# A hybrid S5, attention and memory block on one core: where S5's working tiles lie, and four rooms for raw weights in the memory stage

## Chip, core and metric

The kernel runs on one core of a Trainium2 chip. The metric is the device time of one execution in microseconds, the median of several runs. Lower is better.

The engines are named as in the profile: PE is TensorE's matmul, PEld its weight load, DVE is VectorE, ACT is ScalarE, POOL is GpSimd, and SP is the queue of SyncE from which almost every DMA of this kernel is issued. All five run their own instructions in order and wait for one another through semaphores.

## What is computed

One decoder layer on a sequence of 512 tokens, width 2048, all in float32:

```
h    = rmsnorm(x, norm_pre)
proj = h @ w_in          # columns: S5 input u, S5 gate, q, k, v, gate of the
                         # differential attention, query and gate of the memory attention
y_s  = s5_scan(u, ...)   # 64 groups of 16 channels, 64 complex states each
y_s  = gelu(y_s); y_s *= sigmoid(y_s @ w_glu + b_glu); y_s *= silu(gate_s)
y_d  = diff_attention(rope(q), rope(k), v) * silu(gate_d)
mem_n = rmsnorm(mem, norm_mem)                       # 256 memory tokens
y_x  = memory_attention(q_x, mem_n @ w_mem_kv) * silu(gate_x)
out  = x + rmsnorm(concat(y_s, y_d, y_x) @ w_out, norm_post)
```

`s5_scan` is a recurrence over the sequence, x_t = a x_(t-1) + b u_t with a complex diagonal a, read out as Re(C x) + D u.

## The kernel before

**Chunks.** All large products are cut into 144 *chunks*. A chunk is one block of weights of 128x1024 floats (512 KB) with the matmuls that use it. Every product is done as three matmuls on split operands: `parts` turns the raw block into a high half (`whi`, a cast on ACT) and a low half (`wlo`, a subtraction on DVE); activations are split the same way into `hhi`/`hlo`, `mhi`/`mlo` (the memory tokens), `ysh`/`ysl` and so on. A full chunk is 24 matmuls of 512 columns. The chunks of the memory stage are half as long: 24 matmuls of 256 columns (`w_kv_a`, eight chunks) or 12 of 512 (`w_kv_b`, eight chunks).

The chunks come in this order:

| chunks | from name | work |
|---|---|---|
| 0-15 | | S5 input u |
| 16-31 | S0 = 16 | keys and values of the memory tokens, the *memory stage* |
| 32-63 | SG = 32 | S5 gate, memory query, memory gate; S5 itself runs beside them |
| 64-71 | S1 = 64 | GLU |
| 72-87 | S2 = 72 | v and gate of the differential attention; memory attention beside them |
| 88-103 | S3 = 88 | k and q, differential attention beside them |
| 104-119 | S4 = 104 | first half of the output projection |
| 120-143 | S5 = 120 | second half, as a product with fewer block multiplications |

**Rooms for weights.** `load` puts a raw block into a tile of tag `raw`, of which there are two. `parts` makes `whi` and `wlo`, three of each. The main loop at the end of `tile_hybrid_block` runs the chunks; before the matmuls of chunk n it calls `load` up to chunk n + 3 and `parts` up to chunk n + 2 (from n = 9 on). A load into a room waits until the `wlo` of the block that was there is done.

**Side work.** Everything else hangs on the chunks through `at_slot(t, f)`: f is traced in chunk t + 0.75 by quarters, so that `at_slot(33.5, f)` comes after the second quarter of chunk 34. The matmuls keep the traced order exactly. DVE and ACT instructions traced after a `parts` call may not overtake it (class `After`). Otherwise a scheduler orders each queue at build time by traced order and by when it takes an instruction to be ready, so a load whose room is free can be put some chunks ahead of its place.

**S5.** The 64 groups are done in eight *octets* of eight groups. In the chunks before 32, `s5_products`, `s5_maps` and `s5_weights` prepare the parameters of every octet and write them to DRAM (`sp_dr`, `k_dr`); they load `bc`, an octet's B and C parameters. u lies in DRAM in `u_dr`. Then, for octet o, with e = SG + 1 + 3.25 o as its base slot:

- `s5_load` brings `sp` (576 KB), `s5_u` brings `us` for two octets in eight DMAs of 64 KB, `s5_toeplitz` brings `tm`;
- `s5_angles` makes cosine and sine (`cs`) on POOL, DVE and ACT; `s5_spread` copies a part of `sp` into the block matrices `ub` on ACT (four copies);
- `s5_states`, in six steps, does 16 matmuls of `us` and `ub` into `ps_s`, then a chain on DVE: rotations through `ra` into `wre` and `wim`, scans into `zre` and `zim`, rotations back into `x`;
- `s5_outputs` does 8 matmuls of `us` and `tm` and 16 of `x` and `sp` into `ps_t`, and then GELU.

The first octet has slots of its own: its states begin at e + 1.5, while those of the others begin at e.

**Memory on the right side.** Tiles of a stage come from pools that are stacked at the high end of SBUF. `mp` holds the memory stage's tiles: first `mhi` and `mlo` (16 KB per partition each, at 147,072 and 163,456), behind them `rmb`, parameters, `rows`, small tiles, the two `mT` tiles in which raw memory tokens arrive (`mem_load`), `mk` and `mv`. `s5_open` (slot SG - 1, the end of chunk 31) closes `mp` and opens `s5w` on the same memory, from 151,648 to 220,320. There the order of the allocations sets the addresses: `ub0`, `ub1`, `tm0`, `x0`, `tm1`, `x1`, then tags `sp`, `us`, `cs`, `ra`, `wre`, `wim`, `zre`, `zim`, `ysb`, `sq`. With `reuse_waits="tile"` a new tile waits for the old tiles that it overlaps, for each of them until its last use. `mhi` and `mlo` are read until the last matmul of chunk 31.

**Two later places.** `x_open` (slot S2 - 1) loads the memory attention's keys and values, `mk_dr` and `mv_dr`, through the two `raw` rooms and splits them. `ys_load(c)` loads two blocks of S5's finished output at slots S4 - 0.75 + c, splits them, and subtracts halves (`n3f`). The differential attention of the last head still runs there; `a_finish` transposes a head's result into `ps_t` and splits it into `ydh` and `ydl`.

Of the kernel before, what the change touches and what calls it, by code (L numbers as in the profile page):

```python
# [10 lines left out]
F32 = mybir.dt.float32  # L11
# [43 lines left out]
def tile_hybrid_block(ctx: ExitStack, tc: tile.TileContext, a: dict, out: bass.AP):  # L55
# [539 lines left out]
    def s5_open():  # L595
        prstack.close()
        mstack.close()
        wk = s5["wk"] = right_pool(s5stack, "s5w")
        s5["ub"] = [wk.tile([P, 4, 2, 64], F32, name=f"ub{i}") for i in range(2)]
        s5["d"] = []  # L600
        for i in range(2):
            d = {"tm": wk.tile([P, 8, P], F32, name=f"tm{i}"), "x": wk.tile([P, 8, NCH + 1], F32, name=f"x{i}")}
            g.memset(d["tm"], 0.0)
            g.memset(d["x"][:, :, 0], 0.0)
            g.memset(s5["ub"][i], 0.0)
            s5["d"].append(d)

    oct_ = [{} for _ in range(8)]

    def t512(tag, bufs=1, shape=(P, 512)):  # L610
        return s5["wk"].tile(list(shape), F32, tag=tag, name=tag, bufs=bufs)

    def s5_load(o):

        sp = t512("sp", 2, (P, 1152))
        sy.dma_start(sp, sp_dr[o])
        oct_[o].update(dp=sp[:, 0:640].rearrange("p (g j h) -> p g j h", g=8, h=16), up=sp[:, 640:1152])

    def s5_u(i, x):

        if x == 0:
            us = t512("us", 2, (P, 8, NCH))
            for k in range(2):
                oct_[2 * i + k]["us"] = us[:, 4 * k:4 * k + 4]
            s5["us"] = us
        src = u_dr[i].rearrange("(q x h) (s c) -> s x h q c", x=2, h=16, s=LCH)
        for b_ in range(LCH):
            r0 = 64 * x + 16 * b_
            sy.dma_start(s5["us"][r0:r0 + 16], src[LCH - 1 - b_, x])
# [9 lines left out]
    def s5_angles(o):  # L639

        cs = t512("cs", 2, (P, 2, 4, P))
# [17 lines left out]
    def s5_states(o):  # L659
# [17 lines left out]
        yield  # L677
        zre, zim = t512("zre"), t512("zim")
        for q in range(4):
# [6 lines left out]
        for i, (y1, y2, op) in enumerate(((zre, zim, ALU.subtract), (zim, zre, ALU.add))):  # L686
            b1, b2 = t512("ra", 2), t512("ra", 2)
            v.tensor_tensor(b1, y1, c_, ALU.mult)
            v.tensor_tensor(b2, y2, s_, ALU.mult)
            for g_ in range(2):  # L690
                rows = slice(64 * g_, 64 * g_ + 64)
                b1_, b2_ = (t_[rows].rearrange("p (q c) -> p q c", q=4) for t_ in (b1, b2))
                v.tensor_tensor(xg[64 * i:64 * i + 64, :, g_, 1:], b1_, b2_, op)
            yield

    def s5_outputs(o):
# [41 lines left out]
    for o in range(8):  # L738
        e = SG + 1 + 3.25 * o
        at_slot(e - 0.75, lambda o=o: s5_angles(o))  # L740
        at_slot(e - 0.5 + (0 if o else 1), lambda o=o: s5_spread(o))
        for i in range(6):
            at_slot(e + STEPS[i] + (0 if o else 1.5), lambda o=o, i=i: (oct_[o].setdefault("st", s5_states(o)), next(oct_[o]["st"])))
        if o > 1:
            at_slot(e - 2.5, lambda o=o: s5_load(o))
            if o % 2 == 0:
                for x in range(2):
                    at_slot(e - 3.25 + 0.75 * x, lambda o=o, x=x: s5_u(o // 2, x))
                    at_slot(e - 4.5 + 0.75 * x, lambda o=o, x=x: s5_toeplitz(o // 2, x))
        at_slot(e + 3.75, lambda o=o: s5_outputs(o))  # L750
    S5_END = SG + 1 + 3.25 * 7 + 4.5
# [49 lines left out]
    def x_open():  # L801
# [589 lines left out]
```

## Time and profile before

| | |
|---|---|
| median of 3 runs | 810.77 us (809.38 to 811.61) |
| the profiled execution | 813.09 us, span 811.3 us |
| mean granted TensorE clock | 0.988 |
| PE busy | 788.2 us, 97% of the span |
| DVE, ACT, POOL busy | 73%, 47%, 10% |
| HBM traffic | 216 GB/s over the span |
| the chain that ended last | PE 73%, DVE 10%, DMA 8%, ACT 4% |

The profile cuts the span into 40 slices and gives busy shares in tenths. PE's 97% says that little is left beside its own work, but a busy PE is not always a fast one: the profile also gives the clock granted to TensorE, and a matmul of 512 columns starts every 0.23 us at the full clock and every 0.43 us behind a longer wait. Matmul rows overlap: a row is 0.39 us long while the next one starts after 0.23, so times are taken from start to start. All instructions that the wrapper `After` issues carry line 71 in the profile and all matmuls line 96, so they are told apart by their tiles.

### The profile page before, as it was taken

To read this page: it belongs to the slowest core of one execution; us is meant where nothing else is said; L and a number is where in the kernel's file an instruction comes from. 1 tells how busy PE (TensorE), PEld (TensorE's weight loads), DVE (VectorE), ACT (ScalarE), POOL (GpSimd) and SP (SyncE) were. 2 spreads that over 40 slices of the span, in tenths; PEclk is the share of its full clock that TensorE was granted. 3 is DMA by queue.
4 is the path that set the end of the run, shared out by engine and by line. 5 is a ranking of instruction groups with operands and counts; after the bars stand their busy time and mean duration, and the time that the engine had idled before them with its cause. 6 is when DMAs were issued, how large, how long until landed. Compare 5 with 4: busy or idle time off the path is not lost.

```text
span 811.3 us, 10986 instructions
## 1 busy us (share of the span) xinstructions
PE 788.2 (97%) x3934; PEld 653.6 (81%) x3934; DVE 590.3 (73%) x1086; ACT 381.4 (47%) x621; POOL 80.3 (10%) x106
## 2 busy tenths in 40 slices
PE   8999999897999999999999999999999999999995
PEld 7888897685888888888887888888888788888884
DVE  5599987538898989856894554557988956775757
ACT  5654433332544445434633443445767644345631
POOL 0000000200000000000121222222211010000001
PEclk9999999898999999999999999999999999999998
DMA  8967876673465655357778766455653425437877
GB/s 262 368 253 260 278 238 228 218 203 93 149 170 147 158 160 147 129 144 243 238 233 271 256 159 179 156 157 181 157 130 104 134 101 182 156 108 242 298 286 259
DMA packets 66918, 158.87 MB, mean 196 GB/s; under 512 B 13616, under 2 KB 26800, under 8 KB 65200
## 3 DMA queue, kind: packets, MB, share of 16 engines
q1 hardware_dynamic: 64048, 141.39, 53.6%
q0 software_dynamic: 2816, 16.78, 8.3%
q8 instruction: 31, 0.51, 0.3%
q14 instruction: 23, 0.19, 0.1%
HBM read 134.68 MB, written 40.24 MB: 216 GB/s over the span
## 4 chain that ended last, share of the span: by engine, by line
PE 73%; DVE 10%; DMA 8%; ACT 4%; issue 3%; SPq 1%; POOL 0%; DVEq 0%; POOLq 0%; ACTq 0%
PE ps_mm L96 59%; PE ps_t L96 7%; PE ps_s L96 6%; DVE wlo L71 3%; ACT whi L71 2%; DMA raw<-in_w_kv_b_dram 2%; DMA raw<-in_w_in_a_dram 2%; PE ps_t L99 1%; DMA raw<-in_w_kv_a_dram 1%; SPq L71 1%; DMA ys_dr<-tg 1%; DMA sp<-sp_dr 1%; DMA raw<-in_w_in_b_dram 1%; DVE xr L71 1%; DMA yr<-ys_dr 1%
## 5 line engine op out<-in xcount | busy, mean ns | idle before, releaser
L71 ACT CAST whi<-raw 128x1024 fp32r<-128x1024 f32 (+1 forms) x135 | 138.8, 1029 | 214.5 <-PE ps_mm L96 94.7
L71 DVE TENSOR_TENSOR wlo<-raw,whi 128x1024 fp32r<-128x1024 f32 (+1 forms) x135 | 161.9, 1201 | 105.7 <-ACT whi L71 105.2
L96 PE MATMUL ps_mm<-hhi,whi 128*128 128x512 f32 x512 | 203.5, 398 | 0.9 <-DVE ut L71 0.4
L96 PE MATMUL ps_mm<-hlo,whi 128*128 128x512 f32 x512 | 200.7, 392 | 0.5 <-DVE hlo L71 0.5
L96 PE MATMUL ps_mm<-hhi,wlo 128*128 128x512 f32 x512 | 200.6, 392 | 0.0
L96 PEld LDWEIGHTS ps_mm<-hhi,whi 128*128 128x128 f32 x512 | 96.9, 189 | 22.5 <-issue 1.5
L96 PEld LDWEIGHTS ps_mm<-hhi,wlo 128*128 128x128 f32 x512 | 96.6, 189 | 20.7
L96 PEld LDWEIGHTS ps_mm<-hlo,whi 128*128 128x128 f32 x512 | 96.7, 189 | 20.2 <-DVE hlo L71 1.2
L1071 POOL COPY anchor<-whi 128x1 f32<-128x1 f32 x32 | 29.6, 925 | 232.2 <-ACT whi L71 232.2
L96 PE MATMUL ps_mm<-wlo,hhi 128*128 128x512 f32 x128 | 50.0, 390 | 0.8 <-DVE wlo L71 0.8
L96 PE MATMUL ps_mm<-whi,hhi 128*128 128x512 f32 x128 | 50.1, 391 | 0.0
L96 PE MATMUL ps_mm<-whi,hlo 128*128 128x512 f32 x128 | 50.0, 390 | 0.0
L96 PEld LDWEIGHTS ps_mm<-wlo,hhi 128*128 128x128 f32 x128 | 24.0, 188 | 5.8 <-DVE wlo L71 1.1
L96 PEld LDWEIGHTS ps_mm<-whi,hlo 128*128 128x128 f32 x128 | 24.0, 188 | 5.1
L96 PEld LDWEIGHTS ps_mm<-whi,hhi 128*128 128x128 f32 x128 | 24.0, 188 | 4.8
L71 ACT ACTIVATE pr<-sm,nm 128x128 f32<-128x128 f32 (+3 forms) x32 | 18.0, 564 | 20.6 <-DVE nm L71 20.6
L71 DVE TENSOR_TENSOR x<-ra 64x512 f32<-64x512 f32 x32 | 26.3, 822 | 0.8
L96 PE MATMUL ps_mm<-whi,ysh 128*128 128x512 f32 x64 | 25.6, 401 | 0.0
L96 PE MATMUL ps_mm<-gehi,whi 128*128 128x512 f32 x64 | 25.3, 395 | 0.0
L96 PE MATMUL ps_mm<-gehi,wlo 128*128 128x512 f32 x64 | 25.3, 395 | 0.0
L96 PE MATMUL ps_mm<-gelo,whi 128*128 128x512 f32 x64 | 25.3, 395 | 0.0
L96 PE MATMUL ps_mm<-whi,ysl 128*128 128x512 f32 x64 | 25.1, 391 | 0.0
(336 smaller groups left out, 1522.1 us busy)
## 6 DMA issues: line engine op xcount, KB each, us to landing
raw<-in_w_in_a_dram SPq DMA_DIRECT2D x63, 512.0 KB, 4.3
raw<-in_w_out_b_dram SPq DMA_DIRECT2D x20, 512.0 KB, 3.3
T<-in_w_out_b_dram POOLq DMA_DIRECT2D x16, 512.0 KB, 6.0
raw<-in_w_in_b_dram SPq DMA_DIRECT2D x16, 512.0 KB, 4.5
sp<-sp_dr SPq DMA_DIRECT2D x8, 576.0 KB, 4.7
rows<-in_x_dram SPq DMA_DIRECT2D x4, 1024.0 KB, 8.0
raw<-in_w_kv_a_dram SPq DMA_DIRECT2D x8, 512.0 KB, 4.8
raw<-in_w_kv_b_dram SPq DMA_DIRECT2D x8, 512.0 KB, 4.2
```

Of the source, the lines that this page charges most:

```text
L71: r = f(*args, **kw)
L96: pin(pe.matmul(*args, **kw))
L99: pin(pe.transpose(o, i, ident))
L1071: m = g.tensor_copy(anchor, now["hi"][:, 0:1])
```

## The change

It consists of five edits.

1. `s5_open` allocates every S5 tile once, in a list `late + early`. `late` (second set of octet tiles, the DVE chain's tiles) comes first and thus at the low addresses; `early` (`sp0`, `us0`, `ub0`, `ub1`, `cs0`, `tm0`, `x0`, `sp1`, `ysb0`, `ysb1`) follows. `turn(tag)` hands out the tiles of a tag in rotation, in place of `t512`, which allocated anew each time. Sizes and numbers of tiles are the same.
2. The slots of the first octet: `s5_spread` at 33 (was 33.5), states from 33.75 (was 34.5), outputs at 37.25 (was 36.75). `s5_load(2)` at 37.75 (was 37).
3. The memory stage: for n from 15 to 28 raw blocks are loaded up to chunk n + 5 (at most 31), and odd blocks 17 to 31 go into tiles of tag `mT`, so that there are four rooms.
4. `x_open` loads `mk_dr` and `mv_dr` into a tile `mraw` of its own.
5. `ys_load(1)`, `(2)` and `(3)` come half a slot later.

```diff
     def s5_open():
...
-        s5["ub"] = [wk.tile([P, 4, 2, 64], F32, name=f"ub{i}") for i in range(2)]
-        s5["d"] = []
-        for i in range(2):
-            d = {"tm": wk.tile([P, 8, P], F32, name=f"tm{i}"), "x": wk.tile([P, 8, NCH + 1], F32, name=f"x{i}")}
+        shapes = {"tm": [P, 8, P], "x": [P, 8, NCH + 1], "ub": [P, 4, 2, 64], "us": [P, 8, NCH], "cs": [P, 2, 4, P],
+                  "sp": [P, 1152], "ysb": [P, 2, 512]}
+        late = ["tm1", "x1", "us1", "cs1", "ra0", "ra1", "wre0", "wim0", "zre0", "zim0", "sq0"]
+        early = ["sp0", "us0", "ub0", "ub1", "cs0", "tm0", "x0", "sp1", "ysb0", "ysb1"]
+        room = {n: wk.tile(shapes.get(n[:-1], [P, 512]), F32, name=n) for n in late + early}
+        s5["turn"] = {t_: itertools.cycle([room[m] for m in sorted(room) if m[:-1] == t_]) for t_ in {n[:-1] for n in room}}
+        s5["ub"] = [room["ub0"], room["ub1"]]
+        s5["d"] = [{"tm": room[f"tm{i}"], "x": room[f"x{i}"]} for i in range(2)]
+        g.memset(s5["ub"][0], 0.0)
+        g.memset(s5["ub"][1], 0.0)
+        for d in s5["d"]:
             g.memset(d["tm"], 0.0)
             g.memset(d["x"][:, :, 0], 0.0)
-            g.memset(s5["ub"][i], 0.0)
-            s5["d"].append(d)
...
-    def t512(tag, bufs=1, shape=(P, 512)):
-        return s5["wk"].tile(list(shape), F32, tag=tag, name=tag, bufs=bufs)
+    def turn(tag):
+        return next(s5["turn"][tag])
...
-        at_slot(e - 0.5 + (0 if o else 1), lambda o=o: s5_spread(o))
+        at_slot(e - 0.5 + (0 if o else 0.5), lambda o=o: s5_spread(o))
         for i in range(6):
-            at_slot(e + STEPS[i] + (0 if o else 1.5), lambda o=o, i=i: (...))
+            at_slot(e + STEPS[i] + (0 if o else 0.75), lambda o=o, i=i: (...))
         if o > 1:
-            at_slot(e - 2.5, lambda o=o: s5_load(o))
+            at_slot(e - (2.5 if o > 2 else 1.75), lambda o=o: s5_load(o))
...
-        at_slot(e + 3.75, lambda o=o: s5_outputs(o))
+        at_slot(e + (3.75 if o else 4.25), lambda o=o: s5_outputs(o))
...
-            split(*xa[nm], load(src))
+            split(*xa[nm], load(src, raw=xp.tile([P, 1024], F32, tag="mraw", name="mraw", bufs=1)))
...
-        at_slot(S4 - 0.75 + c, lambda c=c: ys_load(c))
+        at_slot(S4 - 0.75 + c + (0.5 if c else 0), lambda c=c: ys_load(c))
...
+    def last_load(n):
+        if n < 9:
+            return n + 2
+        if 15 <= n < SG - 3:
+            return min(n + 5, SG - 1)
+        return min(n + 3 if n < S5 - 2 else n + 5, S6 - 1)
+
+    def raw_room(m):
+        if S0 < m < SG and m % 2:
+            return mp.tile([P, 1024], F32, tag="mT", name="rawm", bufs=2)
+        return late_raw() if m > S5 and m % 2 else None
+
     for n, (_, f) in enumerate(chunks):
-        while len(raws) <= min(n + 2 if n < 9 else n + 3 if n < S5 - 2 else n + 5, S6 - 1):
+        while len(raws) <= last_load(n):
             m = len(raws)
-            raws.append(load(chunks[m][0], raw=late_raw() if m > S5 and m % 2 else None))
+            raws.append(load(chunks[m][0], raw=raw_room(m)))
```

More of the change, by code (lines that the diff above doesn't have):

```diff
@@ L1 @@
+import itertools
 import math
@@ L597, in s5_open @@
         mstack.close()
-        wk = s5["wk"] = right_pool(s5stack, "s5w")
-        s5["ub"] = [wk.tile([P, 4, 2, 64], F32, name=f"ub{i}") for i in range(2)]
-        s5["d"] = []
-        for i in range(2):
-            d = {"tm": wk.tile([P, 8, P], F32, name=f"tm{i}"), "x": wk.tile([P, 8, NCH + 1], F32, name=f"x{i}")}
+        wk = right_pool(s5stack, "s5w")
+        shapes = {"tm": [P, 8, P], "x": [P, 8, NCH + 1], "ub": [P, 4, 2, 64], "us": [P, 8, NCH], "cs": [P, 2, 4, P],
[9 more added lines that the diff above has]
+        for d in s5["d"]:
             g.memset(d["tm"], 0.0)
             g.memset(d["x"][:, :, 0], 0.0)
-            g.memset(s5["ub"][i], 0.0)
-            s5["d"].append(d)
     oct_ = [{} for _ in range(8)]
-    def t512(tag, bufs=1, shape=(P, 512)):
-        return s5["wk"].tile(list(shape), F32, tag=tag, name=tag, bufs=bufs)
+    def turn(tag):
+        return next(s5["turn"][tag])
     def s5_load(o):
-        sp = t512("sp", 2, (P, 1152))
+        sp = turn("sp")
         sy.dma_start(sp, sp_dr[o])
@@ L621, in s5_u @@
         if x == 0:
-            us = t512("us", 2, (P, 8, NCH))
+            us = turn("us")
             for k in range(2):
@@ L639, in s5_angles @@
     def s5_angles(o):
-        cs = t512("cs", 2, (P, 2, 4, P))
+        cs = turn("cs")
         an, kr = cs[:, 0], cs[:, 1]
@@ L667, in s5_states @@
         yield
-        a1, a2, a3, a4 = t512("ra", 2), t512("ra", 2), t512("ra", 2), t512("ra", 2)
-        wre, wim = t512("wre"), t512("wim")
+        a1, a2, a3, a4 = turn("ra"), turn("ra"), turn("ra"), turn("ra")
+        wre, wim = turn("wre"), turn("wim")
         v.tensor_tensor(a1, vre, c_, ALU.mult)
@@ L677, in s5_states @@
         yield
-        zre, zim = t512("zre"), t512("zim")
+        zre, zim = turn("zre"), turn("zim")
         for q in range(4):
@@ L686, in s5_states @@
         for i, (y1, y2, op) in enumerate(((zre, zim, ALU.subtract), (zim, zre, ALU.add))):
-            b1, b2 = t512("ra", 2), t512("ra", 2)
+            b1, b2 = turn("ra"), turn("ra")
             v.tensor_tensor(b1, y1, c_, ALU.mult)
@@ L708, in s5_outputs @@
         if o % 2 == 0:
-            s5["y"] = t512("ysb", 2, (P, 2, 512))
+            s5["y"] = turn("ysb")
         ysb = s5["y"]
-        sq = t512("sq")
+        sq = turn("sq")
         s.activation(sq, yp, AF.Square)
@@ L740, in tile_hybrid_block @@
         at_slot(e - 0.75, lambda o=o: s5_angles(o))
-        at_slot(e - 0.5 + (0 if o else 1), lambda o=o: s5_spread(o))
+        at_slot(e - 0.5 + (0 if o else 0.5), lambda o=o: s5_spread(o))
         for i in range(6):
-            at_slot(e + STEPS[i] + (0 if o else 1.5), lambda o=o, i=i: (oct_[o].setdefault("st", s5_states(o)), next(oct_[o]["st"])))
+            at_slot(e + STEPS[i] + (0 if o else 0.75), lambda o=o, i=i: (oct_[o].setdefault("st", s5_states(o)), next(oct_[o]["st"])))
         if o > 1:
-            at_slot(e - 2.5, lambda o=o: s5_load(o))
+            at_slot(e - (2.5 if o > 2 else 1.75), lambda o=o: s5_load(o))
             if o % 2 == 0:
```

## The prediction

> **What bounds the kernel now.** I read the page's engine table and clock line first, then PE's waits, then stretches of 5 us, then the timelines of the engines around each wait. PE rows are start, length, operation, and in brackets the idle time before it with its releaser.
>
> ```profile
> PE 788.2 (97%) x3934; PEld 653.6 (81%) x3934; DVE 590.3 (73%) x1086; ACT 381.4 (47%) x621; POOL 80.3 (10%) x106
> PEclk9999999898999999999999999999999999999998
> ...
> PE ps_t L96 <- DVE x L71: 5.9, 2, 5.0
> PE ps_s L96 <- ACT whi L71: 2.1, 1, 2.1
> PE ps_t L99 <- DVE ydl L71: 1.6, 1, 1.6
> ...
> PE ps_s L96 <- DVE wlo L71: 1.0, 2, 0.8
> PE ps_mm L96 <- DVE wlo L71: 0.8, 1, 0.8
> ...
> 521.00 32.67 PE ps_mm L96 x144
> ```
>
> TensorE bounds the kernel: 97% busy, and in an undisturbed stretch 144 matmuls take 32.67 us, 0.227 each, so a chunk of 24 takes 5.45. Time is to be had only where PE waits, or where a wait drops its clock: the two slices with an 8 in the clock line. The waits named are few: 5.9 for S5's x, 2.1 + 1.0 for weight halves in the memory stage, 1.6 for ydl, 0.8 for wlo. The change touches all four places.
>
> The memory stage:
>
> ```profile
> 143.84 0.40 PE L96 MATMUL ps_s<-whi,mlo 128*128 128x512 f32 x1
> 146.35 0.50 PE L96 MATMUL ps_s<-whi,mhi 128*128 128x512 f32 x1 [2.12 <-ACT whi L71]
> 147.61 0.80 PE L96 MATMUL ps_s<-wlo,mhi 128*128 128x512 f32 x1 [0.76 <-DVE wlo L71]
> ...
> 153.75 0.41 PE L96 MATMUL ps_s<-whi,mhi 128*128 128x512 f32 x1
> 145.00:150.00 5.00, 2.89 (x7) 2.09 (x8) 3.67 (x5) 2.62 (x4) 0.00 (x0) 0.69 0.40 132
> 139.59 1.22 DVE L71 TENSOR_TENSOR wlo<-raw,whi 128x1024 fp32r<-128x1024 f32 x1
> 140.39 0.94 SPq L71 DMA_DIRECT2D raw<-in_w_kv_b_dram  x2
> 145.25 1.04 ACT L71 CAST whi<-raw 128x1024 fp32r<-128x1024 f32 x1 [7.42 <-DMA raw<-in_w_kv_b_dram]
> raw<-in_w_kv_b_dram SPq DMA_DIRECT2D x8, 512.0 KB, 4.2
> ```
>
> From 143.84 to 153.75 PE starts 16 matmuls in 9.91 us; at 0.227 they are 3.63, so 6.3 us are lost: 2.12 + 0.76 idle, the rest because the granted clock (third column from the end) fell to 0.69 in these 5 us and stayed low behind the idle. A raw room turns over in about 0.47 (issue) + 4.2 (landing) + 1.04 + 1.22 = 6.9 us. With two rooms that is 3.5 per chunk, and PE wants a chunk of twelve 512-wide matmuls every 2.7 us plus small work. The lead runs out.
>
> S5's first octet:
>
> ```profile
> 155.90 0.95 POOL L603 MEMSET tm<- 128x1024 f32 x1 [49.09 <-PE ps_s L96]
> 165.09 0.33 SPq L71 DMA_DIRECT2D raw<-in_w_in_a_dram  x1
> 165.52 0.38 SPq L71 DMA_DIRECT2D sp<-sp_dr  x1
> 172.56 0.41 ACT L71 COPY ub<-sp 64x256 f32<-64x256 f32 x1 [3.71 <-DMA sp<-sp_dr]
> 175.99 1.95 PE L96 MATMUL ps_s<-us,ub 128*128 128x128 f32 x16
> 184.54 1.23 DVE L71 TENSOR_TENSOR wlo<-raw,whi 128x1024 fp32r<-128x1024 f32 x1 [3.13 <-ACT whi L71]
> 197.13 2.13 DVE L71 TENSOR_TENSOR x<-ra 64x512 f32<-64x512 f32 x2
> 191.87 1.05 PE L96 MATMUL ps_t<-us,tm 128*128 128x128 f32 x8
> 205.10 0.40 PE L96 MATMUL ps_mm<-hhi,whi 128*128 128x512 f32 x1
> 218.21 1.78 PE ps_s L96 x16
> ...
> 222.75 1.92 PE ps_t L96 x24
> ```
>
> From 191.87 to 205.10 PE does 24 output matmuls and 9 of the chunk in 13.23 us. Undisturbed they take 1.92 (the second octet's row) + 9 x 0.227 = 3.96, so 9.3 are lost: 5.9 idle, 3.4 behind it. The cause begins at 155.90: POOL's first clearing waits for the stage's last ps_s matmul, since the new tiles lie on the split tokens. sp is issued only at 165.52, lands at about 172.5, and ACT, in order, holds the next weight half behind the ub copies. That frees raw rooms late, and DVE idles 3.13 for a weight half in the middle of the octet's chain.
>
> **The change part by part.**
>
> *Tiles and loads.* No instruction of S5 is added or dropped. By their sizes, the eleven tiles of the first list cover 30,752 bytes from 4,576 above mhi's start, just past mlo's end; sp0, us0, ub, cs0, tm0, x0 and sp1 lie behind, on rooms that are done earlier. So 576 + 512 + 576 KB (1.7 MB) can go out before the stage ends. This adds those bytes to its last third, at the best rate below (380 GB/s) 4.5 us of all DMA engines, beside a mean share of 0.69. Cost: 0 to 4.5, taken 1.0, near the low end since 31% of 56.5 us is free.
>
> ```profile
> 99.30:155.80 56.50, 53.28 (x389) 45.84 (x388) 41.48 (x62) 19.21 (x26) 0.70 (x1) 0.94 0.69 226
> 20.00:30.00 10.00, 10.00 (x46) 8.28 (x45) 6.05 (x8) 5.60 (x7) 0.00 (x0) 1.00 1.01 380
> ```
>
> *Slots of octet 0.* Its states move from the second quarter of chunk 35 to the third of chunk 34, 18 matmuls earlier; its outputs move 12 matmuls later. Between them now stand 84 chunk matmuls and two state groups, 84 x 0.227 + 2 x 1.78 = 22.6 us, with 1.0 of us,tm work ahead of the first x: 23.6. The chain used (197.13 + 2.13) - 175.99 = 23.3 with its holes; without DVE's 3.13 it needs 20.2. Even unimproved it just fits, if the states start on time. They are now due 66 matmuls plus 0.8 of transposes, 15.8 us, after the stage's end; before, PE had its ub 20.1 after it (175.99, the memset's 155.90 marking the end). Loads issued ahead of 155.9 remove those 4.3 and more. Gain: 0 to 9.3, taken 9.3. sp for octet 2 and the outputs are moved alike, so SP holds at the same place as before: nothing. The tiles kept in a fixed rotation have the same counts as the rotating ones, and although the second octets' tiles now lie under the GLU inputs, octet 7's outputs end some 3.5 chunks, 19 us, ahead of the GLU's first chunk, which hides eight short splits: nothing, and a few us of PE if that lead were gone.
>
> *Four raw rooms.* 6.9 us over four rooms is 1.7 per chunk, below 2.7. Gain: 0 to 6.3, taken 6.3, as nothing else in the stage held PE for more than 0.2. The price is the fourth block of tokens. It shares the mT rooms, and now comes behind chunk 17's raw there:
>
> ```profile
> 95.30 1.22 DVE L71 TENSOR_TENSOR wlo<-raw,whi 128x1024 fp32r<-128x1024 f32 x1
> 105.85 0.28 PE L96 MATMUL ps_mm<-mhi,whi 128*128 128x256 f32 x1
> 112.01 0.28 PE L96 MATMUL ps_mm<-mhi,whi 128*128 128x256 f32 x1
> ```
>
> This wlo (chunk 17) frees the room at 96.5, the block (512 KB, as a raw) lands at about 100.7 and is split by about 103; chunk 20, starting at 112.01, needs it in its second half. What queues behind it on ACT is whi of chunk 18, due as both halves by 105.85: a wait of 0 to 4, taken 1.0.
>
> *Own room for mk and mv.*
>
> ```profile
> 422.94 0.32 SPq L71 DMA_DIRECT2D raw<-mv_dr  x1
> 426.53 6.07 SPq L71 DMA_DIRECT2D raw<-in_w_in_b_dram  x2
> ```
>
> Both took ring rooms, so chunk 75's weights left at 426.53 and PE waited 0.8. With the ring free they go out when mk did. mv now waits for mk's split on SP, but its values are wanted chunks later. Gain 0 to 0.8, taken 0.8.
>
> *ys_load half a slot later.*
>
> ```profile
> 634.86 0.68 DVE L71 TENSOR_TENSOR ysl<-yr,ysh 128x512 fp32r<-128x512 f32 x1
> 637.01 0.68 DVE L71 TENSOR_TENSOR ydl<-ps_t,ydh 128x512 fp32r<-128x512 f32 x1
> ```
>
> From 634.86 DVE does 2.1 us of ys work directly ahead of the ydl that PE waits 1.6 for; moved behind it, the wait goes. DVE is full there, so the work is only reordered. Gain 0 to 1.6, taken 1.6.
>
> Sum: 6.3 + 9.3 + 0.8 + 1.6 = 18.0, less 1.0 and 1.0 = 16.0 us. The profiled execution (813.1 us, 2.3 above the median) would be 797.1; against the median of 810.8 that is **794.8**.
>
> **A rule against a row.** Behind 2.12 + 0.76 us of idle, with one matmul between, the clock fell to 0.69, while the 1.6 us wait for ydl left no trace in the clock line; I price a wait of 2.9 at 6.3. The Trainium skill, "TensorE: Matmul & The Clock Gate", section "Part 1: The HAM clock gate", has the clock halve only after an idle window of about 3.4 us. By that rule this stall would be worth its 2.9 alone, the sum 12.6, the time 798.2; the trace disagrees, and the row decides.
>
> **The rivals.**
>
> *The loads stay late* (the change doesn't do what it says at S5). SP is one queue in order; before, sp stood behind three raws that waited for DVE. If that order persists, ub is again ready 20.1 after the stage and PE waits 4.3 at the states, plus the 3.4 of slow clock: 7.7 lost instead of 9.3. 794.8 + 7.7 = 802.5. For it: sp at 165.52 right behind raw at 165.09. Against: nothing ties sp to the tokens any more.
>
> *The memory stage is held by DMA, not by rooms.* If it keeps its 56.5 us at 226 GB/s, 6.3 stays lost and the allowance of 1.0 for it is moot: 794.8 + 6.3 - 1.0 = 800.1. For it: 1.7 MB more. Against: 380 GB/s was reached, and the 7.42 us hole on ACT follows loads issued only when rooms fell free.
>
> *Slower: raws block SP ahead of bc.* Loads five chunks ahead may wait for rooms at SP's head, with the parameter loads bc behind them; DVE, in order, then holds wlo behind bp.
>
> ```profile
> 117.79 0.42 SPq L71 DMA_DIRECT2D bc<-in_bc_dram  x1
> 129.21 0.69 DVE L71 TENSOR_TENSOR bp<-w,bc 128x512 f32<-128x512 f32 x1
> bc<-in_bc_dram SPq DMA_DIRECT2D x8, 256.0 KB, 3.9
> ```
>
> The slack is 129.21 - 117.79 - 3.9 = 7.5 us. Past that, each of four octets could cost a stall like the measured one: 4 x 6.3 = 25.2 in a stage that I forecast free of stalls, so 794.8 + 25.2 - 1.0 = 819.0. It decides once three octets are late (18.9 against the sum of 16.0). Against: bc precedes most raws' room waits today too.
>
> **How the numbers follow.** Forecast 0.63; late loads 0.15; DMA-bound 0.12; SP blocked 0.06; both gains of S5 and the memory stage failing together (about 808 to 812) 0.04. The likeliest alone spans 792 (no allowance: 792.8, with the runs' spread) to 798. The range 792 to 803.5 takes in both milder rivals, about 0.83. A measurement of this kernel can tell about 0.3%, 2.4 us, from no change. Faster: 0.63 + 0.15 + 0.12 = 0.90; same 0.04; slower 0.06.
>
> **What would show it.** Right: no PE wait for whi or wlo in the memory stage, and clock 1.00 through it; sp and us issued ahead of the stage's last matmul; the states near 16 us after it; no wait for x; mv's load no longer between in_w_in_b raws that PE needs; no wait for ydl. Wrong: PE waiting for ub at the states, whi of chunk 18 behind the fourth token block, bc behind raws on SP, or a new drop in the clock line.

## The result, and the profile after

The changed kernel takes **805.7 us** (median of 6 runs, 804.1 to 808.1), the kernel before 811.0 in the same series (809.4 to 813.8). The ratio is 0.9941, with a 95% interval of 0.9915 to 0.9967: faster, by 5.4 us and not by 16.0. The profiled execution of the changed kernel has a span of 806.3 us, that of the kernel before 811.3: 5.0 us between the two. These two are compared below. Both are among the longest of their series, so that one stretch can be a microsecond or two above its usual length. Helper lines have moved by one (L71 is now L72, L96 is L97).

The page of the changed kernel, TensorE's row and the granted clock in 40 slices:

```profile
PE 786.4 (98%) x3934; PEld 652.2 (81%) x3934; DVE 590.7 (73%) x1086; ACT 381.4 (47%) x621; POOL 80.4 (10%) x106
...
PEclk9999999999999999999998999999999999999998
```

The two slices of 8 among the 9s (around 150 and 190 us) are gone, and a new one has come around 430 us. TensorE's waits in the changed kernel (total, times, longest):

```profile
PE ps_s L97 <- ACT qh L72: 2.8, 1, 2.8
PE ps_s L97 <- ACT ub L72: 2.2, 3, 1.0
PE ps_t L97 <- DVE rm L72: 1.6, 1, 1.6
PE ps_mm L97 <- DVE ut L72: 1.5, 1, 1.5
```

Every wait that the prediction set out to remove has left the list: no x, no ydl, no weight half of `ps_s`, and none in the v rows (a wait of 0.6 for wlo that is still there belongs to another chunk, at 107.89). Four others have come or grown: qh (the high half of the memory attention's query), ub, rm (the scale of the memory tokens' norm) and ut (an S5 input on its way to DRAM). Where the time went is seen by cutting the span at the first matmul of each stretch in TensorE's timeline. The marks of the changed kernel:

```profile
129.59 0.39 PE L97 MATMUL ps_s<-whi,mhi 128*128 128x512 f32 x1
153.36 0.40 PE L97 MATMUL ps_s<-whi,mlo 128*128 128x512 f32 x1
206.71 1.95 PE L97 MATMUL ps_s<-us,ub 128*128 128x128 f32 x16
363.90 0.40 PE L97 MATMUL ps_mm<-gehi,whi 128*128 128x512 f32 x1
408.71 0.40 PE L97 MATMUL ps_mm<-whi,hhi 128*128 128x512 f32 x1
618.96 0.39 PE L97 MATMUL ps_mm<-whi,yxh 128*128 128x512 f32 x1
633.38 0.39 PE L97 MATMUL ps_mm<-whi,ysh 128*128 128x512 f32 x1
```

They are: kv_b's first matmul, the memory stage's last, the states of octet 2, the GLU, the v rows, the output projection, and its first use of ys. The lengths between them, and the same for the kernel before, in us:

| stretch | before | changed | difference | predicted |
|---|---|---|---|---|
| start to kv_b | 124.64 | 129.59 | +4.95 | +1.0 (fourth block) |
| kv_b | 30.97 | 23.77 | -7.20 | -6.3, +1.0 (traffic) |
| stage's end to octet 2's states | 62.44 | 53.35 | -9.09 | -9.3 |
| octet 2's states to GLU | 154.62 | 157.19 | +2.57 | 0 |
| GLU to v rows | 44.80 | 44.81 | 0 | 0 |
| v rows to output projection | 204.79 | 210.25 | +5.46 | -0.8 |
| to the first use of ys | 16.11 | 14.42 | -1.69 | -1.6 |
| to the last matmul | 163.95 | 163.92 | 0 | 0 |

Two lengths of the kernel before vary from one profiled execution to the next. The three kernels below that keep its two raw rooms take 28.52, 29.60 and 30.61 us for kv_b, and one of them (mk's own tile alone), whose code is the same up to octet 2, takes 60.16 us and not 62.44 from the stage's end. The ten with four rooms take 23.76 to 23.80 for kv_b. So the gains of 7.2 and 9.1 us are measured from the longest of these; from the shortest they would be 4.8 and 6.8.

The three large gains came almost to the number: 18.0 us together. 13.0 us went in three other stretches, two of which the prediction had priced at +1.0 and -0.8, and one at nothing.

*The start.* Timelines of SP, ScalarE and TensorE, changed kernel:

```profile
97.66 0.33 SPq L72 DMA_DIRECT2D mT<-in_memT_dram  x1
103.47 1.71 ACT L72 ACTIVATE mhi<-mT,cols 128x256 fp32r<-128x256 f32 x4 [3.69 <-DMA mT<-in_memT_dram]
...
107.58 1.05 ACT L72 CAST whi<-raw 128x1024 fp32r<-128x1024 f32 x1
...
107.89 0.38 PE L97 MATMUL ps_mm<-mhi,wlo 128*128 128x256 f32 x1 [0.62 <-DVE wlo L72]
110.88 0.65 PE L97 MATMUL ps_t<-dp,bp 128*32 128x64 f32 x16 [1.58 <-DVE rm L72]
```

```profile
110.00:115.00 5.00, 4.12 (x36) 3.98 (x37) 4.77 (x9) 1.03 (x2) 2.55 (x3) 0.66 1.01 330
```

The fourth token block goes out at 97.66, once chunk 17's split has freed the room, and is there at 103.4. ScalarE idles 3.69 us for it with whi of chunks 18 to 20 behind. DVE waits for the same block, and then has its split, ut and two wlo halves ahead of rm; TensorE waits 0.62 and 1.58, and the granted clock of the five microseconds from 110 is 0.66 (third column from the end).

*The memory attention.* First mk's load in the kernel before, then timelines of SP, ScalarE and TensorE in the changed kernel, and a window of it:

```profile
418.99 0.32 SPq L71 DMA_DIRECT2D raw<-mk_dr  x1
```

```profile
410.27 0.33 SPq L72 DMA_DIRECT2D raw<-in_w_in_b_dram  x1
...
415.94 0.32 SPq L72 DMA_DIRECT2D ys_dr<-tg  x1
416.31 0.43 SPq L72 DMA_DIRECT2D subln<-in_subln_dram  x1
416.85 0.38 SPq L72 DMA_DIRECT2D mraw<-mk_dr  x1
...
426.38 1.04 ACT L72 CAST mkh<-mraw 128x1024 fp32r<-128x1024 f32 x1 [10.90 <-DMA mraw<-mk_dr]
...
428.00 0.53 PE L97 MATMUL ps_s<-mkh,qh 128*128 128x256 f32 x1 [2.78 <-ACT qh L72]
```

```profile
431.00:436.00 5.00, 5.00 (x15) 3.92 (x15) 2.75 (x5) 2.64 (x4) 0.94 (x2) 0.61 0.56 202
```

The weights of the v rows now stand where mk and mv stood: they leave 1.6 and 5.5 us after the first matmul of the v rows (410.27 and 414.21 against 408.71), as mk and mv did before (418.99 and 422.94 against 417.47). mk's load, in its own tile, leaves 8.1 us after that matmul, behind the last ys write, and its split starts 9.5 us later; before, it left after 1.5 and was split 3.2 us later. So the split is 13.0 us later against TensorE, 6.6 by the issue and 6.4 by the landing. ScalarE stands 10.9 us with the query's split and a weight half behind it, TensorE waits 2.78, and then only 15 matmuls start in five microseconds at a clock of 0.61.

*Octets 3 and 7.* ScalarE's timeline at octet 7 in the kernel before, then in the changed kernel, and TensorE's waits at both octets there:

```profile
323.98 1.66 ACT L71 COPY ub<-sp 64x256 f32<-64x256 f32 x4
325.66 1.28 ACT L71 ACT_TABLE_LOAD   x1
```

```profile
313.71 1.28 ACT L72 ACT_TABLE_LOAD   x1
315.00 0.63 ACT L72 ACTIVATE cs<-cs 128x512 f32<-128x512 f32 x1
315.54 0.39 ACT L72 COPY ub<-sp 64x256 f32<-64x256 f32 x1
...
230.23 1.83 PE L97 MATMUL ps_s<-us,ub 128*128 128x128 f32 x14 [0.98 <-ACT ub L72]
318.40 1.83 PE L97 MATMUL ps_s<-us,ub 128*128 128x128 f32 x14 [0.97 <-ACT ub L72]
```

At octet 7 the four copies into ub came ahead of the table load and the sines before; now ScalarE takes the sines first and among the copies, and TensorE waits for the copies. At octet 3 two of the four copies already stood among the sines before, with a wait of 0.52 us; now all four come behind the first sine, and the waits are 0.25 and 0.98.

### The profile page after: what moved, and what is told of

It is laid out like the page before. It is cut to its first block, busy times and chain, and to the rows that moved or that the text cites. A ratio compares the mean times of both kernels' runs of the same rounds, so it can differ in the third digit from the quotient of the medians.

```text
span 806.3 us, 10995 instructions
## 1 busy us (share of the span) xinstructions
PE 786.4 (98%) x3934; PEld 652.2 (81%) x3934; DVE 590.7 (73%) x1086; ACT 381.4 (47%) x621; POOL 80.4 (10%) x106
## 4 chain that ended last, share of the span: by engine, by line
PE 78%; DVE 9%; DMA 6%; ACT 3%; issue 2%; SPq 1%; POOL 0%; DVEq 0%; POOLq 0%; ACTq 0%
PE ps_mm L97 60%; PE ps_s L97 9%; PE ps_t L97 7%; DVE wlo L72 2%; DMA raw<-in_w_in_a_dram 1%; PE ps_t L100 1%; DMA mraw<-mk_dr 1%; DMA rows<-in_x_dram 1%; DMA par<-in_par_dram 1%; DMA ys_dr<-tg 1%; DVE sm L72 1%; ACT whi L72 1%; SPq L72 1%; DMA mT<-in_memT_dram 1%; DVE xr L72 1%
## 5 line engine op out<-in xcount | busy, mean ns | idle before, releaser
L72 ACT CAST whi<-raw 128x1024 fp32r<-128x1024 f32 (+1 forms) x127 | 130.6, 1029 | 182.5 <-PE ps_mm L97 106.8
L72 DVE TENSOR_TENSOR wlo<-raw,whi 128x1024 fp32r<-128x1024 f32 (+1 forms) x127 | 152.3, 1201 | 82.5 <-ACT whi L72 82.0
L97 PE MATMUL ps_mm<-hhi,whi 128*128 128x512 f32 x512 | 202.4, 395 | 2.1 <-DVE ut L72 1.5
L97 PE MATMUL ps_mm<-hlo,whi 128*128 128x512 f32 x512 | 199.9, 390 | 0.5 <-DVE hlo L72 0.4
L97 PE MATMUL ps_mm<-hhi,wlo 128*128 128x512 f32 x512 | 199.8, 390 | 0.0
L97 PEld LDWEIGHTS ps_mm<-hhi,whi 128*128 128x128 f32 x512 | 96.2, 188 | 23.4 <-DVE ut L72 1.9
L97 PEld LDWEIGHTS ps_mm<-hhi,wlo 128*128 128x128 f32 x512 | 96.1, 188 | 20.7
L97 PEld LDWEIGHTS ps_mm<-hlo,whi 128*128 128x128 f32 x512 | 96.2, 188 | 20.3 <-DVE hlo L72 1.6
L1079 POOL COPY anchor<-whi 128x1 f32<-128x1 f32 x32 | 27.6, 862 | 241.2 <-ACT whi L72 241.2
L97 PE MATMUL ps_mm<-whi,hhi 128*128 128x512 f32 x128 | 50.9, 398 | 0.0
L97 PE MATMUL ps_mm<-wlo,hhi 128*128 128x512 f32 x128 | 50.7, 396 | 0.0
L97 PE MATMUL ps_mm<-whi,hlo 128*128 128x512 f32 x128 | 50.6, 396 | 0.0
L97 PEld LDWEIGHTS ps_mm<-whi,hlo 128*128 128x128 f32 x128 | 24.6, 192 | 5.3
L97 PEld LDWEIGHTS ps_mm<-whi,hhi 128*128 128x128 f32 x128 | 24.6, 192 | 4.9
L97 PEld LDWEIGHTS ps_mm<-wlo,hhi 128*128 128x128 f32 x128 | 24.6, 192 | 4.9
L72 DVE TENSOR_TENSOR ra<-ps_s,cs 128x512 f32<-128x512 f32 x32 | 20.9, 685 | 7.2 <-PE ps_s L97 3.5
L72 ACT ACTIVATE pr<-sm,nm 128x128 f32<-128x128 f32 (+3 forms) x32 | 18.1, 564 | 16.8 <-DVE nm L72 16.6
L97 PE MATMUL ps_mm<-whi,ysh 128*128 128x512 f32 x64 | 25.6, 400 | 0.0
L97 PE MATMUL ps_mm<-gehi,whi 128*128 128x512 f32 x64 | 25.3, 395 | 0.0
L97 PE MATMUL ps_mm<-gehi,wlo 128*128 128x512 f32 x64 | 25.3, 395 | 0.0
L97 PE MATMUL ps_mm<-gelo,whi 128*128 128x512 f32 x64 | 25.3, 395 | 0.0
L97 PE MATMUL ps_mm<-whi,ysl 128*128 128x512 f32 x64 | 25.1, 392 | 0.0
```

Source lines behind the costliest of these rows:

```text
L72: r = f(*args, **kw)
L97: pin(pe.matmul(*args, **kw))
L1079: m = g.tensor_copy(anchor, now["hi"][:, 0:1])
```

## The experiments

Stretches are those of the table above, from each kernel's profiled execution. Medians are of six runs where no count is given; ratios are to the kernel before on the same chip.

### The fourth block ahead of chunk 17's raw

```
-        at_slot(8.5 + 2 * i, lambda i=i: (mem_load(i), mem_split(i)))
+        at_slot(8.5 + 2 * i if i < 3 else 13, lambda i=i: mem_load(i))
+        at_slot(8.5 + 2 * i, lambda i=i: mem_split(i))
```

> The changed kernel, with the load of the fourth block of memory tokens asked for at slot 13, ahead of chunk 17's raw weights in the ring of two rooms that both use (its split stays at slot 14.5). Theory (order in the ring): of the changed kernel's 805.7 us the 3.9 us that kv_a loses between 100 and 130 come from this block, issued at 97.7 and landed at 103.4, at which ScalarE and VectorE wait in order with whi of chunks 18 to 20 behind them. With the block ahead that goes: 801.8 us (800.5 to 803.0), no ScalarE wait for mT over 1 us, and kv_b starts near 125.5 instead of 129.6. Rival (traffic): the added raw loads fill the DMA engines, and whichever of the two transfers goes second is late: chunk 17's raw then holds ScalarE instead, and the time stays within 805 to 806.5.

Measured: **802.1 us** (799.8 to 804.2), ratio 0.9897 (0.9860 to 0.9935). Timelines of SP and ScalarE, and the window of kv_a up to kv_b's start:

```profile
78.79 0.33 SPq L72 DMA_DIRECT2D mT<-in_memT_dram  x1
...
96.22 1.71 ACT L72 ACTIVATE mhi<-mT,cols 128x256 fp32r<-128x256 f32 x4
```

```profile
99.00:125.00 26.00, 26.00 (x257) 25.21 (x256) 23.71 (x37) 10.62 (x15) 2.65 (x5) 1.00 0.88 285
```

The block leaves 18.9 us earlier, ScalarE splits it without waiting, and TensorE is busy for all of the window at full clock; kv_b starts at 124.88. The DMA engines are at 0.88 there on the mean and deliver 285 GB/s, more than the 257 of the changed kernel from 99 to 129 us, and TensorE waits for none of it. So it was the order in the ring. The price is not a fixed one: among the kernels of this study with four raw rooms, kv_b starts at 129.59, 128.13, 127.29 and 127.90 with the old order (the changed kernel and three below), and at 124.82 to 126.51 with the new one (six kernels). Between the means, 128.2 and 125.4, lie 2.8 us; the changed kernel's profiled execution is the latest of all. The four with the old order all wait for rm, 0.6 to 1.6 us; none of the six with the new one does.

### mk and mv through the ring again

```
-            split(*xa[nm], load(src, raw=xp.tile([P, 1024], F32, tag="mraw", name="mraw", bufs=1)))
+            split(*xa[nm], load(src))
```

> The changed kernel with mk and mv loaded through the two-room ring for raw weights again, as before. Theory (late issue): mk's load in its own tile goes out behind the last ys write and subln, 6.6 us later against TensorE than before, and TensorE, ScalarE and VectorE wait at the first scores of the memory attention; that step lost 5.6 us. Undone: 805.7 - 5.6 + the 0.8 us that the kernel before waits there, 800 to 801.5 us, and the wait for qh or mkh at the first scores is under 1 us. Rival (traffic): the transfers around 410 to 427 are slow whatever the order; then mk lands late in the ring too, a raw of the v rows waits behind it, and the time is 804.5 to 807.

Measured: **801.0 us** (799.9 to 802.2), ratio 0.9884 (0.9847 to 0.9921). Timelines and a window:

```profile
408.42 0.32 SPq L72 DMA_DIRECT2D raw<-mk_dr  x1
...
423.65 0.28 PE L97 MATMUL ps_s<-mkh,qh 128*128 128x256 f32 x1
```

```profile
426.00:436.00 10.00, 10.00 (x48) 8.37 (x47) 5.77 (x11) 3.02 (x6) 3.05 (x4) 1.00 0.89 256
```

mk leaves 1.1 us after the first matmul of the v rows (407.29 here) instead of 8.1, and the first scores wait for nothing. The stretch from the v rows takes 203.58 us instead of 210.25. With its place ahead of the last two ys writes back, mk also lands sooner, 5.3 us after its issue and not 9.5. The DMA engines are at 0.89 in this window and TensorE waits for nothing. So the loss comes from where the load stands on SP. How much of the slow landing is due to the loads that leave beside it, and how much to traffic from elsewhere, no run separates. Over all kernels of this study the stretch takes 203.6 to 205.5 us with mk in the ring (ten kernels) and 209.1 to 210.3 with its own tile (four): between the means, 204.9 and 209.6, lie 4.7 us.

### Both

The two diffs above together.

> Both of the edits above in one: the fourth block ahead of chunk 17's raw, and mk and mv through the ring of raw weights. Theory (two losses in places 300 us apart, which add): 805.7 - 3.9 - 4.8 = 797.0 us (795.5 to 798.5). Rival (traffic, or a loss that only moves on to a later stage): 801 or more.

Measured: **798.6 us** (797.4 to 799.3), ratio 0.9853 (0.9817 to 0.9889), just above what was expected. kv_b starts at 125.17, the stretch from the v rows takes 204.92. The losses are separate and nearly add.

### The tile for mk off the GLU activation

```
+            mraw = xp.tile([P, 1024], F32, tag="mraw", name="mraw", bufs=1)
             xa[nm] = [xp.tile([P, 1024], F32R, name=f"{nm}{x}") for x in "hl"]
-            split(*xa[nm], load(src, raw=xp.tile([P, 1024], F32, tag="mraw", name="mraw", bufs=1)))
+            split(*xa[nm], load(src, raw=mraw))
```

> The changed kernel, with the tile for mk's and mv's raw values given its place ahead of mk's split instead of behind it, so that it no longer shares 128 bytes with the first GLU activation, and mk's load no longer waits for a matmul of the GLU. The order of SP's transfers is the same as in the changed kernel: the load stays behind the last ys write and subln. Theory (order on SP's queue sets the issue): 805.2 to 806.2 us, mk's load still issued near 417. Rival (the place over the GLU activation holds it back): mk goes out about as early as before against TensorE, and the time is 800 to 802 us.

Measured: **805.3 us** (799.4 to 808.3, 12 runs), ratio 0.9917 (0.9887 to 0.9948). Timeline of SP:

```profile
413.60 0.32 SPq L72 DMA_DIRECT2D ys_dr<-tg  x1
...
414.44 0.43 SPq L72 DMA_DIRECT2D mraw<-mk_dr  x1
```

By its new place the tile shares no memory with the GLU activation any more, and mk's load still leaves 8.0 us after the v rows begin (406.44 here), behind the last ys write and the small subln load; ScalarE idles 10.62 us for it. Its place in SP's order holds it; the shared 128 bytes do not. Why the built order puts it there, and not where the ring's load stands, was not tried.

### The edits one at a time

mk's own tile alone, on the kernel before:

```
-            split(*xa[nm], load(src))
+            split(*xa[nm], load(src, raw=xp.tile([P, 1024], F32, tag="mraw", name="mraw", bufs=1)))
```

> The kernel before with one edit of the change alone: mk's and mv's raw values in a tile of their own. Theory (late issue): the load goes out behind the last ys write and subln, as in the changed kernel; from the v rows to the end of the memory attention the changed kernel took 210.25 us and the one before 204.79, so 811.1 + 5.4 = 816.5 us (814.5 to 818): slower. Rival (the edit is harmless by itself and loses only beside the rest of the change, where the stages before it end earlier): 810.3 to 812.

Measured: **815.7 us** (810.6 to 818.5, 12 runs), ratio 1.0058 (1.0036 to 1.0079): this edit is a loss by itself. mk's load leaves 7.7 us after the v rows begin (414.97 here), ScalarE idles 10.85 us for it, and TensorE waits 2.73:

```profile
434.21 0.38 PE L96 MATMUL ps_s<-mkh,qh 128*128 128x256 f32 x1 [2.73 <-ACT qh L71]
```

The four raw rooms alone, on the kernel before (with `last_load` and `raw_room` as in the change):

```
-            raws.append(load(chunks[m][0], raw=late_raw() if m > S5 and m % 2 else None))
+            raws.append(load(chunks[m][0], raw=raw_room(m)))
```

> The kernel before with one edit alone: four rooms for raw weights in the memory stage, with loads up to five chunks ahead. Theory: kv_b shrinks from 31.0 to 23.8 us (7.2), and the fourth token block behind chunk 17's raw takes 0 to 4 of it back in kv_a; S5's first octet keeps its waits. 811.1 - 7.2 + 2 = 806 us (804 to 808). Rival (the traffic of the prefetch bounds the stage): kv_b stays above 29 and the time is 810 to 812.

Measured: **804.0 us** (803.6 to 807.4), ratio 0.9918 (0.9888 to 0.9948). kv_b takes 23.80 us, as in the changed kernel. The timelines of SP and TensorE:

```profile
157.45 0.49 SPq L71 DMA_DIRECT2D sp<-sp_dr  x1
...
191.37 0.43 PE L96 MATMUL ps_t<-x,sp 128*64 128x128 f32 x2 [2.34 <-DVE x L71]
```

With S5's tiles still on the split tokens, sp leaves at 157.45, 5.7 us behind the stage's last matmul (151.70); before, it was 9.9 (165.52 behind 155.61). The raw rooms brought it forward. That alone gains little: the stretch to octet 2's states takes 59.90 us, against 60.16 with mk's own tile alone. TensorE still starts the first octet's states 20.4 us after the stage's end, without a wait, as in both kernels with two rooms and the old slots, because the old slot puts them there.

The new layout and the moved slots alone, on the kernel before (`room`, `turn` and the slots as in the change):

```
-        sp = t512("sp", 2, (P, 1152))
+        sp = turn("sp")
...
-            at_slot(e + STEPS[i] + (0 if o else 1.5), ...)
+            at_slot(e + STEPS[i] + (0 if o else 0.75), ...)
```

> The kernel before with the new layout of S5's tiles and the moved slots alone. Theory: from the memory stage's end to the first GLU chunk the kernel before took 217.06 us and the changed one 210.54, 9.1 gained at the first octet and 2.6 lost at octets 3 and 7, where ScalarE takes the sines ahead of the copies into ub. So 811.1 - 6.5 = 804.6 us (803 to 806). Rival (the layout alone is not enough, since with two raw rooms the loads of sp and us stay behind raws on SP): the states start more than 18 us after the stage's last matmul, and the time is 807 to 811. Rival (the loss at octets 3 and 7 comes from the rest of the change): 801.5 to 802.5.

Measured: **810.4 us** (807.7 to 813.5, 12 runs), ratio 0.9987 (0.9965 to 1.0008): no change to be seen. Timelines of SP and TensorE:

```profile
164.15 0.33 SPq L72 DMA_DIRECT2D raw<-in_w_in_a_dram  x1
164.53 0.42 SPq L72 DMA_DIRECT2D sp<-sp_dr  x1
...
173.14 0.46 PE L97 MATMUL ps_s<-us,ub 128*128 128x128 f32 x2 [3.18 <-ACT ub L72]
```

The tiles are free, and sp leaves right behind a raw that waited for a room, 11.0 us after the stage's last matmul (153.51). The states, moved to an earlier slot, wait 3.18 us for ub. The first rival given was the right one; I had taken the layout's gain as independent of the rooms. The stretch to octet 2's states takes 59.33 us.

The moved slots alone, on the kernel before:

```
-        at_slot(e - 0.5 + (0 if o else 1), ...)
+        at_slot(e - 0.5 + (0 if o else 0.5), ...)
-            at_slot(e + STEPS[i] + (0 if o else 1.5), ...)
+            at_slot(e + STEPS[i] + (0 if o else 0.75), ...)
-            at_slot(e - 2.5, lambda o=o: s5_load(o))
+            at_slot(e - (2.5 if o > 2 else 1.75), lambda o=o: s5_load(o))
-        at_slot(e + 3.75, lambda o=o: s5_outputs(o))
+        at_slot(e + (3.75 if o else 4.25), lambda o=o: s5_outputs(o))
```

> The kernel before with the moved slots alone: S5's tiles as before, two raw rooms, mk, mv and ys as before. Theory (the slots pay only when ub is ready in time, and that is the raw rooms' doing, not the layout's): sp's load still leaves SP behind a raw that waits for a room, TensorE waits about 3 us for ub at the first octet's states, and the time is that of layout and slots together, 810.4, less up to 1.6 for octet 7: 808.5 to 811 us. Rival (the layout brings part of it): without it the states start still later, over 813 us.

Measured: **808.4 us** (806.6 to 811.4, 9 runs), ratio 0.9973 (0.9954 to 0.9992). sp leaves at 165.41, behind a raw at 164.99; the states wait for the tile `us`:

```profile
173.81 0.46 PE L96 MATMUL ps_s<-us,ub 128*128 128x128 f32 x2 [1.45 <-DMA us<-u_dr]
```

The time is just under the range that was expected, and the mechanism was not the expected one. sp leaves 9.5 us after the stage's end, as late as before, and TensorE waits 1.45 us for the tile `us` and 0.43 for ub, where some 3 us were expected. No wait for x is left, and the stretch to octet 2's states takes 55.73 us: in this execution the slots alone bring 4.4 of the 6.8 us that the changed kernel gains there over mk's own tile alone (60.16 to 53.35). By the medians, with two raw rooms the slots gain 2 to 3 us, and the layout on top of them nothing (810.4).

### The ub copies ahead of the sines

On the kernel with both edits (798.6 us):

```
-        at_slot(e - 0.5 + (0 if o else 0.5), lambda o=o: s5_spread(o))
+        at_slot(e - (1 if o in (3, 7) else 0.5) + (0 if o else 0.5), lambda o=o: s5_spread(o))
```

> The changed kernel with the fourth block ahead of chunk 17's raw, mk and mv through the ring (both as in the earlier run of the two edits, 798.6 us), and the copies into ub asked for half a slot earlier at octets 3 and 7, so that ScalarE takes them ahead of the sines. Theory: the waits for ub at octets 3 and 7, 0.25 + 0.98 + 0.97 us with some slow clock, 2.6 in all, go: 796.0 us (795 to 797.2). Rival (ScalarE's work is only reordered): the sines are late instead, VectorE and with it the outputs of these octets wait, and the time stays at 798 to 799.2.

Measured: **795.2 us** (794.5 to 795.6, 4 runs), ratio 0.9798 (0.9765 to 0.9830). The stretch from octet 2's states to the GLU takes 153.86 us instead of 157.18, and no wait for ub is left. The kernel before took 154.62, with its wait at octet 3.

### Which part the first octet's gain comes from

The 795.2 us kernel with the old layout:

```
-        sp = turn("sp")
+        sp = t512("sp", 2, (P, 1152))
```

and the same for every other tile of S5.

> The 795.2 us kernel (fourth block first, mk and mv through the ring, copies into ub earlier at octets 3 and 7) with S5's tiles laid out as before, so that the first octet's tiles lie on the split memory tokens again; slots, raw rooms and the rest stay. Theory (the layout does nothing: sp's load keeps its place on SP behind mv's second write, which comes after the stage's last matmul anyway, and what brought it forward was that no raw on SP waits for a room any more): 794.3 to 796.3 us, the states 16.3 us after the stage's last matmul. Rival (the layout is what lets the loads go early): the states come 18 us or more after the stage's end and the first octet waits for x, 798 to 802 us.

Measured: **795.4 us** (793.8 to 796.8), ratio 0.9799 (0.9774 to 0.9825). Timelines of SP and TensorE:

```profile
154.21 0.52 SPq L71 DMA_DIRECT2D sp<-sp_dr  x1
...
164.89 1.95 PE L96 MATMUL ps_s<-us,ub 128*128 128x128 f32 x16
```

With the tiles back on the tokens the states start 16.3 us after the stage's last matmul (148.59), as in the changed kernel, and the stretch to octet 2's states takes 53.39 us against 53.35. The layout is worth nothing here.

The 795.2 us kernel with the old slots (the diff of the moved slots, turned round):

> The 795.2 us kernel with the first octet's work, the loads of octet 2 and the outputs of octet 0 at their slots of before; layout, raw rooms and the rest stay. Theory (the slots are what turns the earlier ub into time): from the stage's end to octet 2's states the kernel with the raw rooms alone took 59.9 us and the 795.2 us kernel 53.35, so 795.2 + 6.5 = 801.7 us (800.5 to 803), with TensorE waiting for x again. Rival (the layout and the early loads shorten the chain by themselves): under 798 us and no wait for x over 1 us.

Measured: **801.1 us** (798.3 to 803.4), ratio 0.9869 (0.9842 to 0.9897). TensorE waits for x again, and the stretch takes 59.94 us. The waits for x, and the timeline of TensorE at the first octet's states:

```profile
PE ps_t L97 <- DVE x L72: 3.2, 1, 3.2
```

```profile
170.64 1.95 PE L97 MATMUL ps_s<-us,ub 128*128 128x128 f32 x16
```

Here the last copy into ub ends at 166.2, 16.0 us after the stage's last matmul (150.27), and the states start 20.4 us after it, without a wait. An early ub is worth nothing until the slot asks for it.

The old layout without the earlier copies:

```
-        at_slot(e - (1 if o in (3, 7) else 0.5) + (0 if o else 0.5), lambda o=o: s5_spread(o))
+        at_slot(e - 0.5 + (0 if o else 0.5), lambda o=o: s5_spread(o))
```

> The 795.4 us kernel without the new layout, and with the copies into ub at octets 3 and 7 asked for at the change's slots again. One look, for which edit lets ScalarE take the sines first. If the moved slots do so by themselves at octet 3 and the layout at octet 7, TensorE waits 1.2 us in two waits for ub at octet 3 and not at octet 7, the stretch from octet 2's states to the first GLU chunk takes 154.9 us. If the slots do both: 157.2 us and three waits. If the layout does both: 153.8 us and no such wait.

One run of 797.2 us; the stretch from octet 2's states to the GLU takes 155.37 us, and the only wait for ub, of 0.98 us, is at octet 3.

So the added wait at octet 3 comes without the layout, and the one at octet 7 with it: 155.37 against the changed kernel's 157.19, 1.8 us. The slots alone and the slots with the layout, both on the kernel before, give the same pair: 155.37 us with one wait at octet 3, and 157.16 with waits at both. Unless the copies are asked for earlier, the layout costs 1.8 us.

## Why the prediction was wrong

The forecast was 794.8 us; the changed kernel takes 805.7. Step by step:

**Own room for mk and mv: the sign was wrong.** Taken +0.8, measured 5.5 us lost between the two profiles, 4.7 by the medians with this edit alone (815.7 against 811.0). The sentence on the weights, "With the ring free they go out when mk did", came true to 0.1 us, and the wait of 0.8 in the v rows went. What failed is a term that the sum does not have: mk's own departure. It was put at nothing, as if a load with a free room kept its place; the prediction named the queue behind mk's split for mv, and looked for no delay of mk. mk's load moved behind the last ys write, 6.6 us later against TensorE, landed 6.4 us more slowly, and held up the query's split on ScalarE.

**The fourth token block: 1.0 taken, about 3 measured** (5.0 in the profiled execution, which includes a wait of 1.5 for ut in an earlier chunk). The chain was read rightly, and it was named as a thing that would make the prediction wrong; but the landing was put at 100.7 and came at 103.4. The block left at 97.66, not at 96.5, and took 5.8 us, not 4.2, and three weight halves stood behind it, not one. The price came near the upper bound of 4. In the profiled execution the waits also lowered the clock; in two other kernels with the old order they did not (the last section), and kv_b starts at 127.9 and 128.1 there and not at 129.6.

**Tiles kept in a fixed rotation, and slots moved: nothing taken, 2.6 measured.** I counted instructions and transfers on SP, and not ScalarE's order. The slots cost 0.8 of it at octet 3, the layout 1.8 at octet 7. The sum of these three failed steps is the whole miss, in the two profiled executions: 5.46 + 0.8, 4.95 - 1.0 and 2.57 make 12.8 us; kv_b's shortening beyond the 6.3, with the traffic that cost nothing, gives 1.9 back, and the spans differ by 5.0 where 16.0 was forecast.

**The first octet: the size came out, the reason did not.** 9.3 predicted, 9.1 measured (6.8 from the shorter of the two executions with the old code there), but the step "Loads issued ahead of 155.9 remove those 4.3 and more" did not happen. Timelines of SP, POOL and ScalarE, changed kernel:

```profile
157.37 0.32 SPq L72 DMA_DIRECT2D mv_dr<-mv  x1
158.08 0.37 SPq L72 DMA_DIRECT2D k_dr<-kz  x1
158.50 0.52 SPq L72 DMA_DIRECT2D sp<-sp_dr  x1
...
153.64 0.96 POOL L613 MEMSET tm<- 128x1024 f32 x1 [25.56 <-PE ps_s L97]
...
167.12 0.41 ACT L72 COPY ub<-sp 64x256 f32<-64x256 f32 x1
```

sp leaves 5.1 us after the stage's last matmul (153.36): SP is in order, and sp stands behind mv's second write, which needs that matmul's result. Nothing ties sp to the tokens, and its place in the queue ties it to the stage's end all the same. The Trainium skill, "DMA: Bandwidth & Descriptors", section "Anatomy of one DMA — SWDGE (gpsimd) path", says, in a passage on transfers that GpSimd issues, that a semaphore wait happens on the issuing sequencer before a transfer is dispatched, and not in the DMA engines; this trace agrees for SP, with sp issued 0.42 us after the write ahead of it. What went is the raw in front of it that waited for a room. ub is there at 167.5, 14.2 us after the end, and the moved slots want it at 16.3.

The 4.3 us mix two things. The prediction took the states' start in the kernel before, 20.1 us after the stage, as the time at which ub came. ub's last copy did end just ahead of it (175.92), but TensorE waited for nothing there: the old slot asks for the states then, and it does so too in the kernel of 801.1 us, where ub is there 4.4 us earlier. Against the 60.16 us of the same code in the kernel with mk's own tile alone, the raw rooms alone gain 0.3, the slots alone 4.4, the slots with the layout 0.8, and rooms and slots together 6.8. So the gain needs both edits, and the moved slots have as much part in it as the earlier load. That 9.1 came so near to 9.3 is in part luck.

**Right:** the memory stage was bound by rooms and not by traffic (7.2 against 6.3, or 4.8 from the shortest kv_b with two rooms, and a clock of 1.00 from 129 to 153 us), and ys (1.7 against 1.6). The ys edit was not run alone; the stretch to the first use of ys takes 14.3 to 14.4 us in the nine kernels that have it and 15.7 to 16.1 in the five that have not. The allowance of 1.0 us for 1.7 MB in the stage's last third was moot, since that traffic does not fall there.

**The rivals.** "The loads stay late" is what the layout and the slots do without the raw rooms: sp leaves 11.0 us after the stage, TensorE waits 3.18 and 0.72 for ub, and the time is 810.4. "Raws block SP ahead of bc" was not seen. A slower mechanism did exist, in a place where I had looked for a gain.

## What to carry to other kernels

A load leaves when its room is free *and* everything ahead of it on its queue has left: find its neighbours in the queue's timeline before and after, and do not argue from the room alone. A tile in a shared ring has a place in the order as well as a room; giving it a room of its own can cost it that place, as it did mk (4.7 us slower by itself). A start without a wait is set by its slot, not by its operand: ask what would move if the operand came earlier. And when two edits meet at one wait, try each without the other: at the first octet the moved slots and the raw rooms made the gain together, neither of them all of it, and the layout, named first in the change, none.

## What the runs showed of the hardware

Waits of TensorE of about 3 us and less slowed its clock several times. 2.78 us at 428 us in the changed kernel is followed by 0.61. In the kernel with layout and slots alone, 3.18 and 0.72 are followed by 0.68 (first row below). But the length of one wait doesn't decide it. In the changed kernel 0.62 and 1.58 around 110 are followed by 0.66; in the kernel with mk through the ring the second wait at the same place is 1.54, the first only 0.20, and the clock stays at 1.00 (second row). With the raw rooms alone it is 0.17 and 1.54, and 1.00 again. So is it behind 0.25 and 0.98 at 230 us, and behind 1.45 and 0.43 in the kernel with the slots alone.

```profile
175.00:180.00 5.00, 5.00 (x22) 4.43 (x21) 1.98 (x3) 1.05 (x1) 0.00 (x0) 0.68 0.61 181
```

```profile
110.00:115.00 5.00, 3.83 (x46) 3.77 (x47) 5.00 (x11) 1.29 (x2) 2.55 (x3) 1.00 0.95 311
```

The Trainium skill, "TensorE: Matmul & The Clock Gate", section "Part 1: The HAM clock gate", gives about 3.4 us of idle as the window for the lower clock; the rows disagree, as in the prediction, and the row near 110 of the changed kernel most, where the longer of the two waits was 1.58 us. What sets the threshold no run here shows.

The other number is the spread of one load, from issue to the start of its split: mk's 512 KB took 3.2 us in the kernel before and 5.3 with the ring restored, where it left between ys writes, and 9.4 to 9.9 where subln, the query and a raw left within about a microsecond of it.
